# Place 1's expert read as whole fp32 values, and place 2 planned first, in a two-layer decoder trunk

## The chip, the core and the metric

The kernel runs on one core of a Trainium2 chip. A core has TensorE (PE in the rows, its weight loads PEld), VectorE (DVE), ScalarE (ACT), GpSimd (POOL) and SyncE (SP), which here issues the DMA transfers of the weights. The metric is the device time of one execution in microseconds, as a median of several runs.

## The reference: what is computed

256 tokens of width 1024 pass through two layers. Layer 0 is a recurrent mixer beside a memory attention, then a dense SwiGLU. Layer 1 is a differential attention beside a memory attention, then a mixture of experts, which is the part that the change touches:

```python
def moe_swiglu(h, w_router, w13, w2):
    logits = (xt @ w_router).astype(jnp.float32)
    top_v, top_e = lax.top_k(logits, TOP_K)          # 2 of 8 experts for each token
    gates = jax.nn.softmax(top_v, axis=-1)
    ...
    def expert_block(args):
        xb, e = args
        gu = xb @ w13[e]                              # 1024 -> 2 x 3584
        return (jax.nn.silu(gu[:, :EXPERT_DIM]) * gu[:, EXPERT_DIM:]) @ w2[e]
```

All values are fp32. An expert's w13 has 1024 x 7168 values and its w2 3584 x 1024; the eight experts together are 352 MB, and each of them is read once.

## The kernel before, in words

**Products.** TensorE takes either fp32 values or fp32r values, a shortened form of fp32. Nearly all products of weights run in fp32r: each operand is split into a high part (`hi`, ScalarE, a copy that rounds to fp32r) and a low part (`lo`, VectorE, the value minus `hi`), and the product is the sum of hi x hi, hi x lo and lo x hi. A few small products (the router, the softmax parts of layer 0 and 1, `fold`) take plain fp32 operands.

**The stream of weights (`Stream`).** Weights come in loads of 1 MB, 128 partitions x 2048 values. A load needs a raw buffer (`free`: raw0 to raw3 and, in the experts, x_hi; four `e` tiles, h3_hi and h3_lo serve once). `split` turns a load into parts and needs room for them (`room`: part0 to part4, x_lo and h1, seven places of 8 KB in a partition): one place for the high part (L124), one for the low part (L106); after the low part the raw buffer is free, and the next DMA is issued into it (L67). A place comes back when TensorE has read its piece. All this is written in program order on every engine: `split` is called whenever TensorE takes a piece, and does as many splits as there is room for at that point of the program. The first pieces of an expert's first stage are split by halves of 1024 columns (L130, L131).

**The experts.** After the router, expert 0 is place 0 (64 tokens); the other seven are ordered by their number of tokens and become places 1 to 7: place 1 has room for 128 + 8 tokens, places 2 to 4 for 128, places 5 to 7 for 64. An expert has seven blocks `j` of 512 hidden columns, each with three stages: gate `g`, up `u` (two loads each, w13) and down `w` (two loads, w2). The sequence of stages is fixed: place 0 and place 2 mixed, then place 3, then place 1 mixed with places 7, 6, 5 (about three of their stages after each of place 1's), then place 4. For places 2 to 4 the tokens are the stationary operand and the weights move, 512 columns at a time, three products (L368 to L370). For places 0, 5, 6, 7 high and low parts of 64 tokens stand side by side in one stationary operand, so two products do (L1276, L1277), and `fold` adds the halves (L1299).

**Place 1 (`run_moving`).** Here the weights are stationary and the tokens move: `xg` holds 136 high and 136 low parts side by side, so that per 128 x 128 tile of w13 one product hi x (hi, lo) of 272 columns (L1365) and one lo x hi of 136 columns (L1366) are needed. A stage has 32 such pairs, and its two loads are split as a `pair`, their pieces taken in turn. Behind them ScalarE copies one sum out of PSUM (L1370), VectorE adds the other (L1372), and SiLU (L1374) or the product with the gate (L1376) follow.

**The order at the start of the experts.** The router's transposes and products (L1005, L1008) end the attention's part; VectorE finds the top 2 (L1039 to L1068), writes the dispatch matrix of place 0 (L1086), `gather_first` collects its tokens (L1224 to L1228), and then `split` starts in earnest. The rest of the plan (`plan`: the order of the places, the dispatch matrices, the gates, the split of the tokens h3 into h3_hi and h3_lo, L1174 and L1175) is done in steps between the stages of place 0, and `gather` for place 2 follows it.

## Time and profile before

| what | value |
|---|---|
| median of 3 runs | 1576.77 us (1576.06 to 1577.21) |
| the profiled execution, its own time | 1579.21 us |
| its span | 1577.4 us |
| TensorE busy | 1533.0 us, 97% of the span |
| VectorE busy | 1239.3 us, 79% |
| ScalarE busy | 1055.8 us, 67% |
| moved by DMA | 451.60 MB, mean 286 GB/s |

TensorE's busy time counts an instruction from its start to its modelled end, and neighbours overlap; so how fast it goes is read from the distance of starts, and what it waits for from the rows that name a releaser. The experts fill the span from about 574 us to the end.

### The profile page before, as it was taken

What the parts mean: (1) busy time and instruction counts of PE and PEld (TensorE: products, weight loads), DVE (VectorE), ACT (ScalarE), POOL (GpSimd) and SP (SyncE); (2) the same over time, 40 slices, a digit from 0 to 9 for tenths busy, and PEclk for the clock granted to TensorE, in tenths of its full rate; (3) what the DMA queues carried; (4) which work ended last, traced back from release to release, by engine and by line L of the source; (5) the groups of instructions that cost most, each with busy time, mean ns of one, the idle gap of its engine ahead of it and who ended that gap; (6) DMA issues with size and microseconds to landing.
All of it is one profiled execution on the core that took longest, in us unless ns stands there. A gap on an engine that the chain in (4) does not pass through costs nothing.

```text
span 1577.4 us, 22581 instructions
## 1 busy us (share of the span) xinstructions
PE 1533.0 (97%) x8697; PEld 1300.5 (82%) x8697; DVE 1239.3 (79%) x1205; ACT 1055.8 (67%) x1142; POOL 31.9 (2%) x60
## 2 busy tenths in 40 slices
PE   8999999999999989999999999999999999999996
PEld 7988999999998857887888888887878787877774
DVE  6678654555757579888999879889899899889876
ACT  5784544444456457877887778778778787877663
POOL 0000000000000111000000000000000000000000
PEclk9999999999999999999999999999999999999998
DMA  9454655555533755999999999999999999999982
GB/s 295 161 187 161 233 183 183 183 182 197 167 128 126 265 206 194 377 377 387 395 389 352 333 324 353 356 377 377 357 339 377 371 373 353 361 371 363 333 307 98
DMA packets 218678, 451.60 MB, mean 286 GB/s; under 512 B 7241, under 2 KB 62610, under 8 KB 218562
## 3 DMA queue, kind: packets, MB, share of 16 engines
q1 hardware_dynamic: 217490, 446.76, 79.2%
q0 software_dynamic: 1072, 3.32, 0.7%
q8 instruction: 70, 1.15, 0.3%
q14 instruction: 46, 0.38, 0.1%
HBM read 449.00 MB, written 1.05 MB: 285 GB/s over the span
## 4 chain that ended last, share of the span: by engine, by line
PE 79%; DVE 10%; ACT 4%; DMA 4%; issue 2%; POOL 0%; POOLq 0%; SPq 0%; DVEq 0%; ACTq 0%
PE mm L368 11%; PE mm L370 11%; PE mm L369 11%; PE acc L369 6%; PE acc L370 6%; PE acc L368 6%; DVE part L106 5%; PE mm L1276 4%; PE mm L1277 4%; PE mm L1365 3%; DMA raw<-in_moe_w 3%; PE acc L1277 3%; PE acc L1276 3%; PE mm L1299 2%; PE mm L1255 1%
## 5 line engine op out<-in xcount | busy, mean ns | idle before, releaser
L124 ACT ACTIVATE part<-raw 128x2048 fp32r<-128x2048 f32 x188 | 359.2, 1914 | 58.9 <-DMA raw<-in_moe_w 21.6
L106 DVE TENSOR_TENSOR part<-raw,part 128x2048 fp32r<-128x2048 f32 x150 | 341.1, 2284 | 16.1 <-PE mm L370 5.5
L131 DVE TENSOR_TENSOR part<-raw,part 128x1024 fp32r<-128x1024 f32 x166 | 201.4, 1223 | 126.2 <-ACT part L130 125.6
L130 ACT ACTIVATE part<-raw 128x1024 fp32r<-128x1024 f32 x166 | 173.1, 1056 | 87.8 <-PE mm L370 47.8
L368 PE MATMUL mm<-x_hi,part 128*128 128x256 f32 x768 | 220.0, 286 | 2.1 <-ACT part L130 2.1
L370 PE MATMUL mm<-x_hi,part 128*128 128x256 f32 x768 | 218.3, 284 | 1.1 <-DVE part L131 1.1
L369 PE MATMUL mm<-x_lo,part 128*128 128x256 f32 x768 | 217.7, 283 | 0.0
L368 PEld LDWEIGHTS mm<-x_hi,part 128*128 128x128 f32 x768 | 147.9, 193 | 5.3 <-ACT part L130 2.6
L370 PEld LDWEIGHTS mm<-x_hi,part 128*128 128x128 f32 x768 | 147.8, 192 | 1.7 <-DVE part L131 1.6
L369 PEld LDWEIGHTS mm<-x_lo,part 128*128 128x128 f32 x768 | 147.8, 192 | 0.7
L1276 PE MATMUL mm<-part,xs 128*128 128x512 f32 x248 | 98.8, 398 | 0.0
L124 ACT ACTIVATE part<-x_hi 128x2048 fp32r<-128x2048 f32 x46 | 88.0, 1914 | 15.2 <-PE mm L1277 4.0
L1277 PE MATMUL mm<-part,xs 128*128 128x512 f32 x248 | 97.9, 395 | 0.0
L368 PE MATMUL mm<-part,xg 128*128 128x512 f32 x240 | 97.1, 404 | 0.0
L369 PE MATMUL mm<-part,xg 128*128 128x512 f32 x240 | 95.2, 397 | 1.8 <-DVE part L106 1.5
L370 PE MATMUL mm<-part,xg 128*128 128x512 f32 x240 | 94.7, 395 | 0.0
L106 DVE TENSOR_TENSOR part<-x_hi,part 128x2048 fp32r<-128x2048 f32 x37 | 84.5, 2285 | 7.5 <-PE mm L1365 2.5
L106 DVE TENSOR_TENSOR x_lo<-raw,h 128x2048 fp32r<-128x2048 f32 x37 | 84.6, 2285 | 5.8 <-PE mm L370 2.8
L106 DVE TENSOR_TENSOR h<-raw,part 128x2048 fp32r<-128x2048 f32 x38 | 86.8, 2284 | 1.6 <-ACT part L124 1.1
L106 DVE TENSOR_TENSOR part<-raw,x_lo 128x2048 fp32r<-128x2048 f32 x37 | 84.5, 2285 | 2.7 <-PE mm L1365 1.1
L124 ACT ACTIVATE x_lo<-raw 128x2048 fp32r<-128x2048 f32 x37 | 70.8, 1914 | 13.9 <-PE mm L1277 5.1
L1365 PE MATMUL mm<-xg,part 128*128 128x272 f32 x320 | 79.6, 335 | 0.0
(513 smaller groups left out, 3489.5 us busy)
## 6 DMA issues: line engine op xcount, KB each, us to landing
raw<-in_moe_w SPq DMA_DIRECT2D x262, 1024.0 KB, 7.3
x_hi<-in_moe_w SPq DMA_DIRECT2D x66, 1024.0 KB, 7.3
raw<-in_ffn_w SPq DMA_DIRECT2D x42, 1024.0 KB, 4.9
raw<-in_a_w_in SPq DMA_DIRECT2D x10, 1024.0 KB, 9.4
raw<-in_mem_w_kv SPq DMA_DIRECT2D x8, 1024.0 KB
raw<-in_w_kv_shared SPq DMA_DIRECT2D x8, 1024.0 KB, 6.1
raw<-in_a_w_out SPq DMA_DIRECT2D x6, 1024.0 KB, 4.8
raw<-in_b_w_q SPq DMA_DIRECT2D x6, 1024.0 KB
```

The lines of the kernel that those rows point to most:

```text
L106: nc.vector.tensor_sub(lo, src, hi.bitcast(F32))
L124: nc.scalar.activation(hi, src, AF.Copy)
L130: nc.scalar.activation(hi, src, AF.Copy)
L131: nc.vector.tensor_sub(lo, src, hi.bitcast(F32))
L368: PE.matmul(o, lhsT=l_hi, rhs=r_hi, start=start, stop=False)
L369: PE.matmul(o, lhsT=l_hi, rhs=r_lo, start=False, stop=False)
L370: PE.matmul(o, lhsT=l_lo, rhs=r_hi, start=False, stop=stop)
L1255: PE.matmul(p[:, k], lhsT=src[:, t, f], rhs=disp[:, t, g0:g0 + ng], start=t == 0, stop=t == 1)
L1276: PE.matmul(o[h], lhsT=w[:, kt], rhs=w_hi[:, i, f], start=a, stop=False)
L1277: PE.matmul(o[h], lhsT=w[:, kt], rhs=w_lo[:, i, f], start=False, stop=z)
L1299: PE.matmul(p[:, i], lhsT=src[:, i * 128:(i + 1) * 128], rhs=fold, start=True, stop=True)
L1365: PE.matmul(p[m], lhsT=w_hi[:, k, f], rhs=x_[:, kt], start=a, stop=False)
```

## The change

Four things change.

1. w13 of place 1 is not split. Its load is handed on as it is (`"raw"`), the raw buffer goes back only when the stage that reads it is over (`held`), and `xg` holds 136 fp32 values (high and low part added, ScalarE and VectorE). A pair of products becomes one fp32 product of 136 columns (L1404 after), the sums need one bank instead of two, and the copies and adds behind them go (L1370, L1372); SiLU and the product with the gate read PSUM.
2. All other loads of the experts but the first stage's are split by 2048 columns as before; the `pair` form is gone.
3. The first three pieces of place 0's first stage are split earlier, by calls written into the router's code (`upper` for the high parts between the two halves of the router's transposes, `lower` for the low parts at three points behind).
4. In `plan`, place 2's dispatch matrix, the split of h3 and place 2's gather come first; the other dispatch matrices come behind, one at a step. `hidden` has one more step between the product with the gate and the split of its result for the places of 64 tokens.

```diff
+    def upper(self):
+        src, _, whole, slot = self.piece()
+        place = self.room.popleft()
+        hi, lo = self.tiles(place, *src.shape[1:], 2)
+        self.nc.scalar.activation(hi, src, AF.Copy)
+        self.uppers.append((hi, lo, src, slot, place))
+
+    def lower(self):
+        hi, lo, src, slot, place = self.uppers.popleft()
+        self.nc.vector.tensor_sub(lo, src, hi.bitcast(F32))
...
     def split(self):
...
+            if not self.half and self.loaded[0][2] == "raw":
+                (src,), _, _, slot = self.loaded.popleft()
+                self.ready.append((src, None, (slot,)))
+                self.load()
+                continue
...
@@ stage_loads
                 else:
                     yield (rows_(moe_w13, p, k * 512, 4, j * 512 + (FFN if kind == "u" else 0), 512), 4, 512,
-                           p in moving, "pair" if p in moving else n > 0)
+                           False, "raw" if p in moving else n in big)
...
@@ the router, the top 2 and the first dispatch
             ln_tail(*ahead[1], gb, h3[:, 1])
+            st.lower()
+        else:
+            for _ in range(3):
+                st.upper()
...
     DVE.tensor_scalar(val, mb, -BIG, BIG, op0=OP.mult, op1=OP.add)
+    st.lower()
...
     dispatch((0, 0, 64), val)
+    st.lower()
...
@@ plan
+        dispatch(*PLACE[2])
+        yield
+        while st.uses(once):
+            yield
+        h3_parts.extend(hp.tile([128, 2, D], F32R, name=f"h3_{s}") for s in ("hi", "lo"))
...
+        yield from gather(4, True, blocks[2])
         for bs in PLACE.values():
             for b in bs:
-                if b[0]:
+                if b[0] not in (0, 2):
                     dispatch(b)
-            if bs[0][0] % 2:
-                yield
+                    yield
...
@@ run_moving
-        x_ = moving[0]
-        v = mw.tile([128, 4, 136], F32, name="sg")
+        x_, held = moving[0], []
+        v = s.take(2, held)
...
-            for k2 in range(2):
-                w_hi, w_lo = s.get()
-                for m in range(2):
-                    f = slice(m * 128, (m + 1) * 128)
-                    for k in range(4):
-                        a, kt = k2 == 0 and k == 0, 4 * k2 + k
-                        z = kt == KT - 1
-                        PE.matmul(p[m], lhsT=w_hi[:, k, f], rhs=x_[:, kt], start=a, stop=False)
-                        PE.matmul(p[m][:, 1], lhsT=w_lo[:, k, f], rhs=x_[:, kt, 0], start=False, stop=z)
+            for m in range(2):
+                f = slice((2 * c + m) * 128, (2 * c + m + 1) * 128)
+                for kt in range(KT):
+                    PE.matmul(p[:, m], lhsT=v[kt // 4][0][:, kt % 4, f], rhs=x_[:, kt], start=kt == 0, stop=kt == KT - 1)
...
-            for m in range(2):
-                ACT.activation(v[:, 2 * c + m], p[m][:, 1], AF.Copy)
-            for m in range(2):
-                DVE.tensor_add(v[:, 2 * c + m], v[:, 2 * c + m], p[m][:, 0])
...
+        for place in held:
+            s.back(place)
+        s.load()
```

On TensorE, at the start of place 1's first stage, the program before holds these rows (`xg` are the tokens, `part`, `h` and `x_lo` are parts of the weights; 128x272 and 128x136 are the moving columns):

```order
L1287 MATMUL mm<-ident,sg 128x128 x4
L1365 MATMUL mm<-xg,part_8206 128x272
L1366 MATMUL mm<-xg,part_8229 128x136
L1365 MATMUL mm<-xg,part_8206 128x272
L1366 MATMUL mm<-xg,part_8229 128x136
```

The changed program holds at the same place:

```order
L1329 MATMUL mm<-ident,sg 128x128 x4
L1404 MATMUL mm<-xg,raw_8082 128x136 x4
L1404 MATMUL mm<-xg,raw_8120 128x136 x4
L1404 MATMUL mm<-xg,raw_8082 128x136 x4
L1404 MATMUL mm<-xg,raw_8120 128x136 x4
L1404 MATMUL mm<-xg,raw_8082 128x136 x4
```

The products read the raw buffers themselves, one where there were two, and both loads of the stage are read from its first products to its last.

On VectorE, at the router's end, the program before holds the following rows (`val` belongs to the top 2, `disp` is place 0's dispatch matrix, `ys` its gathered tokens; L131 are the low parts of halves of a load, L106 those of whole loads):

```order
L1067 TENSOR_SCALAR val<-mb 128x16
L1068 TENSOR_TENSOR val<-val,mm 128x16
L1086 TENSOR_SCALAR disp<-slots,val 128x64 x2
L1228 TENSOR_TENSOR ys_5466<-mm,ys_5466 128x2x64 x2
L1228 TENSOR_TENSOR ys_5466<-mm,ys_5466 128x4x64
L131 TENSOR_TENSOR part_5492<-x_hi,part_5492 128x1024
L131 TENSOR_TENSOR part_5497<-x_lo,part_5497 128x1024
L131 TENSOR_TENSOR part_5500<-x_lo,part_5500 128x1024
L106 TENSOR_TENSOR h_5505<-raw_5095,part_5503 128x2048
```

And the changed program (a third L117 stands 15 rows further up, ahead of the top 2):

```order
L1100 TENSOR_SCALAR val<-mb 128x16
L117 TENSOR_TENSOR part_5369<-x_lo,part_5369 128x1024
L1102 TENSOR_TENSOR val<-val,mm 128x16
L1120 TENSOR_SCALAR disp<-slots,val 128x64 x2
L117 TENSOR_TENSOR part_5371<-x_lo,part_5371 128x1024
L1267 TENSOR_TENSOR ys_5477<-mm,ys_5477 128x2x64 x2
L1267 TENSOR_TENSOR ys_5477<-mm,ys_5477 128x4x64
L138 TENSOR_TENSOR h_5505<-raw_5095,part_5503 128x2048
```

The three low parts of half loads moved from behind the gathered tokens to three points ahead of them.

On SyncE, in the part where place 1 is mixed with the others, every DMA of the program before waits for VectorE; in the changed program two of them at each w13 stage of place 1 wait for TensorE (the DMAHW names count transfers, PE and DVE name the engine that frees the buffer):

```order
L66 DMA raw_8688<-in_moe_w 128x4x512 [waits DMAHW1_49,PE_49]
...
L66 DMA x_hi<-in_moe_w 128x4x512 [waits DMAHW2_49,PE_49]
...
L66 DMA raw_8703<-in_moe_w 128x4x512 [waits DMAHW6_49,DVE_49]
...
L66 DMA raw_8719<-in_moe_w 128x4x512 [waits DMAHW7_49,DVE_49]
...
L66 DMA raw_8740<-in_moe_w 128x2x1024 [waits DMAHW0_49,DVE_49]
```

What frees the buffers of place 1's w13 moved from VectorE's low part to the end of the stage on TensorE.

## Rows read from the trace of the kernel before

**Rows 1.** The page: the span, and the chain of work that ended last, followed back from the end, as shares of the span by engine and by line.

```profile
span 1577.4 us, 22581 instructions
...
PE 79%; DVE 10%; ACT 4%; DMA 4%; issue 2%; POOL 0%; POOLq 0%; SPq 0%; DVEq 0%; ACTq 0%
PE mm L368 11%; PE mm L370 11%; PE mm L369 11%; PE acc L369 6%; PE acc L370 6%; PE acc L368 6%; DVE part L106 5%; PE mm L1276 4%; PE mm L1277 4%; PE mm L1365 3%; DMA raw<-in_moe_w 3%; PE acc L1277 3%; PE acc L1276 3%; PE mm L1299 2%; PE mm L1255 1%
```

**Rows 2.** Busy time of each engine in four stretches (start and end in us, length, then each engine's busy time and instructions, the granted clock of TensorE, the DMA share and GB/s): the middle of the start of the experts, places 0 and 2, place 1 with 7, 6 and 5, and place 4.

```profile
592.00:616.00 24.00, 22.01 (x100) 17.51 (x100) 22.25 (x32) 16.61 (x19) 7.68 (x20) 0.86 0.26 97
626.00:813.00 187.00, 185.19 (x862) 150.35 (x861) 167.06 (x93) 149.12 (x113) 0.00 (x0) 1.00 1.03 384
937.00:1425.00 488.00, 474.16 (x2657) 398.34 (x2656) 436.40 (x342) 384.18 (x375) 2.09 (x4) 1.00 0.99 363
1425.00:1553.00 128.00, 128.00 (x554) 97.73 (x553) 110.07 (x71) 89.81 (x70) 0.00 (x0) 1.00 0.89 315
```

**Rows 3.** What TensorE waited for between 937 and 1425 us: the first and the last of the eight rows, which are fifteen waits together (us in total, times, longest).

```profile
PE acc L1277 <- DVE part L106: 4.8, 5, 1.3
...
PE acc L369 <- DVE part L106: 2.7, 4, 1.1
...
PE acc L369 <- DVE x_lo L106: 0.5, 1, 0.5
```

**Rows 4.** TensorE in order of time around one of these waits (start, duration, line; in brackets the idle time before it and what ended it).

```profile
1089.70 0.40 PE L1277 MATMUL mm<-h,xs 128*128 128x512 f32 x1
1089.93 0.40 PE L1276 MATMUL acc<-x_lo,hs 128*128 128x512 f32 x1
1091.48 0.50 PE L1277 MATMUL acc<-part,hs 128*128 128x512 f32 x1 [1.15 <-DVE part L106]
1091.82 0.40 PE L1276 MATMUL acc<-x_lo,hs 128*128 128x512 f32 x1
```

**Rows 5.** VectorE's low parts (L106) and ScalarE's high parts (L124) of whole loads between 937 and 1425 us, each as one row: busy time and number.

```profile
937.00:1425.00 488.00, 377.76 (x169) 1.00 0.99 363
...
937.00:1425.00 488.00, 319.88 (x169) 1.00 0.99 363
```

**Rows 6.** The copies and adds behind place 1's products in the same stretch (busy us, mean ns of one, idle before them).

```profile
L1372 DVE TENSOR_TENSOR sg<-sg,mm 128x136 f32<-128x136 f32 x56 | 14.6, 291 | 7.3 <-ACT sg L1370 7.2
...
L1370 ACT ACTIVATE sg<-mm 128x136 f32<-128x136 f32 x56 | 13.6, 275 | 9.2 <-PE mm L1366 9.1
```

**Rows 7.** TensorE in order of time in a stage of place 1 that waits for nothing; from the first row to the last there are eight pairs.

```profile
1084.01 0.34 PE L1365 MATMUL mm<-xg,h 128*128 128x272 f32 x1
1084.19 0.23 PE L1366 MATMUL mm<-xg,x_lo 128*128 128x136 f32 x1
...
1085.92 0.34 PE L1365 MATMUL mm<-xg,part 128*128 128x272 f32 x1
```

**Rows 8.** Products of two plain fp32 operands with a weight load each time, in order of time: the attention's weights times values, 128 moving columns, and the last expert's scatter, 512 moving columns. Each product stands as two MATMULs (x2).

```profile
511.80 0.39 PE L937 MATMUL mm<-vd,wt 128*128 128x128 f32 x2
...
513.14 0.28 PE L937 MATMUL mm<-vd,wt 128*128 128x128 f32 x1
...
1562.50 1.02 PE L1545 MATMUL mm<-us,sh 128*128 128x512 f32 x2
1563.36 1.02 PE L1545 MATMUL mm<-gs,sh 128*128 128x512 f32 x2
```

**Rows 9.** Transfers: issues between 937 and 1425 us with KB each and the median us from issue to landing; the same for the dense layer's weights over the whole span; and GB/s in 40 slices of the stretch from 590 to 616 us.

```profile
raw<-in_moe_w SPq DMA_DIRECT2D x135, 1024.0 KB, 7.2
...
raw<-in_ffn_w SPq DMA_DIRECT2D x42, 1024.0 KB, 4.9
...
GB/s 293 410 410 403 410 400 384 384 384 391 388 350 69 9 0 0 0 0 0 0 25 0 0 0 0 0 0 0 0 0 0 0 0 0 0 0 0 0 0 0
```

**Rows 10.** VectorE in order of time at the router's end (as rows 4).

```profile
564.54 0.36 DVE L1039 SCALAR_TENSOR_TENSOR lg<-mm,rstd,b_rt 128x8 f32<-128x8 f32 x2 [1.83 <-PE mm L1008]
...
569.59 0.17 DVE L1068 TENSOR_TENSOR val<-val,mm 128x16 f32<-128x16 f32 x1 [2.00 <-PE mm L1065]
...
571.68 0.29 DVE L1228 TENSOR_TENSOR ys<-mm,ys 128x128 fp32r<-128x128 f32 x1 [1.46 <-ACT ys L1227]
...
575.37 1.22 DVE L131 TENSOR_TENSOR part<-x_hi,part 128x1024 fp32r<-128x1024 f32 x1 [0.52 <-ACT part L130]
576.51 2.35 DVE L131 TENSOR_TENSOR part<-x_lo,part 128x1024 fp32r<-128x1024 f32 x2
579.07 2.29 DVE L106 TENSOR_TENSOR h<-raw,part 128x2048 fp32r<-128x2048 f32 x1 [0.20 <-ACT part L124]
```

**Rows 11.** ScalarE in order of time there.

```profile
561.90 1.09 ACT L1006 ACTIVATE vd<-mm 128x512 f32<-128x512 f32 x2 [3.30 <-PE mm L1005]
...
574.28 1.05 ACT L130 ACTIVATE part<-x_hi 128x1024 fp32r<-128x1024 f32 x1
575.23 2.00 ACT L130 ACTIVATE part<-x_lo 128x1024 fp32r<-128x1024 f32 x2
577.13 1.91 ACT L124 ACTIVATE part<-raw 128x2048 fp32r<-128x2048 f32 x1
```

**Rows 12.** What TensorE waited for between 574 and 626 us, the first and the last of seven rows.

```profile
PE mm L1277 <- DVE part L106: 3.1, 2, 2.0
...
PE mm L1276 <- ACT part L130: 0.4, 1, 0.4
```

**Rows 13.** SyncE's issues of transfers in order of time after 580 us (x4 with the time from the first to the last).

```profile
581.38 10.85 SPq L67 DMA_DIRECT2D raw<-in_moe_w  x4
615.85 0.37 SPq L67 DMA_DIRECT2D x_hi<-in_moe_w  x1
```

More of the change, by code (lines that the diff above doesn't have):

```diff
@@ L87, in uses @@
         return any(slot in slots for slot in list(self.free) + [l[3] for l in self.loaded] +
-                   ([self.half[3]] if self.half else []))
+                   ([self.half[3]] if self.half else []) + [u[3] for u in self.uppers] +
+                   [place for r in self.ready for place in r[2]])
     def tiles(self, place, n, m, parts):
@@ L95, in tiles, with piece @@
         return t.rearrange("p (s a b) -> s p a b", s=parts, a=n)
+    def piece(self):
+        todo, cols, whole, slot = self.loaded[0]
+        src = todo.pop(0)
+        if not todo:
+            self.loaded.popleft()
+        return src, cols, whole, None if todo else slot
+    def upper(self):
+        src, _, whole, slot = self.piece()
+        assert whole is False
+        place = self.room.popleft()
[5 more added lines that the diff above has]
+        self.nc.vector.tensor_sub(lo, src, hi.bitcast(F32))
+        if slot:
+            self.back(slot)
+        self.ready.append((hi, lo, (place,)))
     def split(self):
@@ L99, in split @@
         self.load()
-        while self.room and not self.hold and (self.loaded or self.half):
-            place = self.room.popleft()
+        while not self.hold and (self.loaded or self.half):
+            if not self.half and self.loaded[0][2] == "raw":
[3 more added lines that the diff above has]
+                continue
+            if not self.room:
+                break
             if self.half:
-                hi, src, cols, slot, first, whole = self.half
+                hi, src, cols, slot, first = self.half
                 self.half = None
+                place = self.room.popleft()
                 lo = self.tiles(place, *src.shape[1:], 1)[0]
@@ L108, in split @@
                 pieces = list(zip(self.halves(hi, cols), self.halves(lo, cols)))
-                pieces = [(*w, (first, place) if w is pieces[-1] else ()) for w in pieces]
-                if whole == "pair" and not self.pair:
-                    self.pair = pieces
-                else:
-                    if self.pair:
-                        pieces = [w for two in zip(self.pair, pieces) for w in two]
-                        self.pair = None
-                    self.ready += pieces
-            else:
-                todo, cols, whole, slot = self.loaded[0]
-                src = todo.pop(0)
-                if not todo:
-                    self.loaded.popleft()
+                self.ready += [(*w, (first, place) if w is pieces[-1] else ()) for w in pieces]
+            else:
+                src, cols, whole, slot = self.piece()
+                place = self.room.popleft()
                 if whole:
@@ L124, in split @@
                     nc.scalar.activation(hi, src, AF.Copy)
-                    self.half = hi, src, cols, slot, place, whole
+                    self.half = hi, src, cols, slot, place
                 else:
-                    if not todo:
-                        self.back(slot)
                     hi, lo = self.tiles(place, *src.shape[1:], 2)
@@ L139, in take @@
             for place in places:
-                self.back(place)
+                if held is None:
+                    self.back(place)
+                else:
+                    held.append(place)
         return [g[:2] for g in got]
@@ L1170, in plan @@
         yield
-        h3_parts.extend(hp.tile([128, 2, D], F32R, name=f"h3_{s}") for s in ("hi", "lo"))
-        hi, lo = h3_parts
-        for t in range(2):
-            ACT.activation(hi[:, t], h3[:, t], AF.Copy)
-            DVE.tensor_sub(lo[:, t], h3[:, t], hi[:, t].bitcast(F32))
-            yield
         for t in range(2):
```

36 lines of the change are left out of this document (25 added, 11 removed).

## The prediction, written before the changed kernel ran

> **What bounds the kernel now.** I read the chain of waits first: four fifths of it are TensorE, a tenth VectorE, and VectorE's largest part is L106, the low parts of the weights [rows 1]. The table by stretches then says where that tenth lies. Place 4 (1425 to 1553 us) has TensorE busy all the time, and nothing in the change touches it. In places 0 and 2 (626 to 813 us) TensorE is idle 187 - 185.19 = 1.8 us. In the stretch of place 1 with 7, 6 and 5 it is idle 488 - 474.16 = 13.8 us, while VectorE is busy 436.4 of 488 us, 89%, and the transfers run at 363 GB/s, under the 384 of the stretch before [rows 2]. All eight rows of TensorE's waits there name VectorE's low parts [rows 3]. So this stretch is TensorE's work, held up by VectorE now and then. The start of the experts (574 to 626 us) is the other place: TensorE waits for splits [rows 12], VectorE is busy 22.25 of 24 us in its middle, and the transfers nearly stop there, because no buffer comes free [rows 2, 13].
>
> **Place 1's products.** A pair of 272 and 136 columns takes (1085.92 - 1084.01) / 8 = 0.239 us from start to start [rows 7]. The stretch has 14 stages x 32 = 448 pairs, 107 us. Each becomes one fp32 product of 136 columns. The trace has no such shape with whole fp32 operands, but its neighbours: with 128 columns six products take 513.14 - 511.80 = 1.34 us, 0.223 us each, and with 512 columns one takes 1563.36 - 1562.50 = 0.86 us [rows 8]. In proportion to the columns 136 would be 0.228 us from the long product and 0.237 us from the short one. I take 0.237, whose shape is nearest: 448 x (0.239 - 0.237) = 0.9 us gained; the bounds are 0.9 and 5 us gained. Below nothing would need a cost that neither neighbour shows; it is a rival below.
>
> The row speaks here against the first impression, that one product for two must be a large gain: the whole product stands as two MATMULs, as the pair did, and its 512 columns take 0.86 us, nearly four times the 0.23 us of an fp32r product of 512 [rows 4]. The Trainium skill ("FP8 and Floating Point Precision", section "TensorE Precision Notes") says that true FP32 makes four passes through the array. The long product agrees (0.86 us for 4 x 512 columns), and by that rule 4 x 136 = 544 columns stand against 408 before, which speaks against the change.
>
> **What the splits cost.** 14 stages x 2 loads = 28 of the 169 loads of the stretch are no longer split. Per load VectorE spends 377.76 / 169 = 2.24 us and ScalarE 319.88 / 169 = 1.89 us [rows 5]: 62.6 and 53.0 us less. The 56 adds (14.6 us) and the 56 copies (13.6 us) go too [rows 6]; SiLU and the product with the gate stay and read PSUM. VectorE's busy time falls from 436.4 to about 359 us, 74% of the stretch, ScalarE's from 384.2 to about 318 us. More than the sum counts where it falls: before, the four parts of a place 1 stage fill four of the seven places, so that at its end only one and a half loads of the next stages stand split. After, all seven places hold the following loads, three and a half of them, and TensorE goes on while VectorE catches up.
>
> What is this worth? Only what TensorE waits: 13.8 us idle, and what each of the fifteen waits [rows 3] adds around it. In the example the starts of two products lie 1.55 us apart, where the distance before was 1089.93 - 1089.70 = 0.23 us, and the next distance is 0.34 us, 0.11 too long: 1.55 - 0.23 + 0.11 = 1.43 us lost for 1.15 us of idle time [rows 4], 0.28 us more. Fifteen times that is 4 us, together 18 us. Some waits will stay: at the rate of places 0 and 2 (1.8 us in 187) 4.7 us in 488, with their additions about 6. So I take 12 us gained in this stretch.
>
> **What it costs.** Place 1's two loads now stay in their raw buffers until the stage is over, 32 x 0.237 = 7.6 us, plus the time that TensorE takes to come to them. Only five buffers serve again and again, so three are left for transfers, and the next DMAs wait for TensorE instead of VectorE. Behind them on SyncE's queue stand the issues into buffers that VectorE frees; these free up only after the stage, since all places are full while it runs, so that the order of the queue alone delays nothing. With a transfer of 7.2 us from issue to landing when several are under way, and 4.9 us where fewer are [rows 9], and eight loads in a cycle of one place 1 stage and three others, the transfers of the next such cycle still come in time: they have about 20 us for eight loads, 8.4 MB, 411 GB/s, just above the 410 of the peaks [rows 9]; cycles with a down stage, and the gathers and scatters between, need less. So this cover is thin. The bounds of the stretch are a gain of 27 us (its 177 MB, 363 x 488, at 384 GB/s would take 461 us) and a loss of 20 us (the rival below).
>
> **The start of the experts.** The three half loads move: on ScalarE into an idle time of 3.30 us before 561.90 [rows 11], where 1.05 + 2.00 us just fit; on VectorE into gaps of 1.83, 2.00 and 1.46 us [rows 10], each longer than the 1.22 us of one. If a gap were too short, the router would be later by the rest, some tenths. The first whole split can then begin on ScalarE at 574.28 instead of 577.13, 2.85 us sooner, and VectorE, which gives the beat until 610 us, follows. Moreover, VectorE's dispatch matrices of all places but place 2, some 3 us, now stand behind ten low parts instead of between them; about 1 us of that I count, since VectorE has to do them all the same soon after. The split of h3 and place 2's gather only change their places within this part. Does the gain hold afterwards? Places 0 and 2 go at TensorE's pace with transfers at 384 GB/s, so the transfers must come sooner too: they do, since x_hi, which was issued again at 615.85 after 24 us without an issue [rows 13], is now split before the four e tiles, and the others follow the same low parts. I take 4 us, with bounds of 0 (the transfers set the pace of the next stretch) and 8 us: all TensorE's waits there, and the clock, 0.86 of full speed between 592 and 616 us, so that a part of it went at the lower of its two levels, 1.2 GHz [rows 2], after a series of waits.
>
> The additional step in `hidden` lets ScalarE do something else while VectorE finishes its product; it costs a beat of which three or more stages are left, so nothing.
>
> **The sum.** 12 + 4 + 0.9 = 17 us. The profiled execution took 1579.2 us, 2.4 us above the median of the runs; it would come to 1562 us, and the median of 1576.8 to 1560 us.
>
> **Rivals.**
> 1. The transfers set the pace of the place 1 stretch. For it speaks the DMA share of 0.99 there; against it that the stretch before moved 384 GB/s over 187 us, and the peaks 410 [rows 2, 9]. Then only the start gains: 1573 us. The Trainium skill ("DMA: Bandwidth & Descriptors", section "Where 436 GB/s comes from") puts the limit of HBM for one core at about 358 GB/s, at which this stretch would be full already; the 384 GB/s do not agree. Chance 0.14.
> 2. Slower: the held buffers starve the transfers. In the 14 stages, 14 x 7.6 = 106 us, one load at a time would be under way, 1.05 MB in 4.9 us, 214 GB/s: 22.7 MB. The other 154 MB at 384 GB/s take 402 us, so the stretch 508 instead of 488 us, and with 4 us from the start 1593 us. It decides as soon as the mean rate of the stretch falls under 363 GB/s. Against it: three buffers stay free, and a place 1 stage needs no transfer of its own while it runs. Chance 0.08.
> 3. Slower: the columns set the price. If the pair's 0.239 us were the price of 408 columns, 544 would take 0.319, and 448 x 0.08 = 36 us more; with 16 us gained elsewhere 1597 us (544 is four times 136, after the nearly four times of the long product). The 0.223 us for 4 x 128 = 512 columns speak against it: the pair is slower than its columns. The rule behind it is the Trainium skill's of four passes, named above. Chance 0.03.
> 4. More: the waits vanish altogether and the start brings its upper bound: 27 + 8 us, down to 1542 us. Chance 0.09.
>
> **How the numbers follow.** The forecast has 0.66, with its own range of 1550 to 1570. The range of 8 in 10 reaches from 1547 to 1577: it takes in rival 1 and the nearer half of rival 4, and leaves the slower ones out. A measurement of this kernel can tell 0.2% from no change, 3.2 us. Faster by more: the forecast, rival 4 and half of rival 1, 0.82; within: the other half of rival 1, 0.07; slower: rivals 2 and 3, 0.11.
>
> **What would show it.** In the profile after: L1404 with 0.23 to 0.24 us from product to product; TensorE's idle time in the stretch of place 1 at 3 to 6 us, with the low parts gone as its releaser; VectorE at about 74% there, 141 low parts; a rate above 370 GB/s; at the start, the first whole low part right behind place 0's gather, about 3 us sooner after the router than before. Wrong would be the forecast if TensorE waited for DMA in place 1's stages, or if SyncE's waits for L1404 were long and the transfers paused in them.

## The result, and the profile after

The changed kernel takes 1589.64 us (median of 4 runs, 1589.15 to 1591.57), the kernel before 1576.49 (4 runs). The ratio is 1.0081 [1.0069, 1.0093] (in brackets, here and below, the 95% interval): slower by 0.8%, where 1560 us, 1.1% faster, was predicted. The profiled executions, 1589.48 and 1579.21 us, lie 10.3 us apart, and so do their spans; the one before lies 2.7 us above its median, so the medians lie further apart, 13.2 us. One profiled execution below, that of the last run on the start, fell in a slower state (1656 us, granted clock 0.85), so its stretches are not read, and its time is the median of the other four.

Where the 10.3 us lie: place 1's first product starts at 937.3 us before and at 930.2 after, so the start of the experts gained 7.1 us. The last product of `fold`, which ends the stretch of places 1, 7, 6 and 5, starts at 1421.2 before and at 1431.5 after: the stretch grew from 483.9 to 501.3 us, by 17.4. Place 4 behind it is as long as before. The rows of these four starts, two before and two after (duration in ns, then the first and the last start in us):

```profile
L1365 PE MATMUL mm<-xg,part x320: 287/338/435, 937.3 to 1365.8; 128*128 128x272 f32 x160
L1299 PE MATMUL mm<-fold,us x208: 217/275/275, 627.1 to 1421.2; 128*128 128x64 f32 x104
```

```profile
L1404 PE MATMUL mm<-xg,raw x672: 277/279/535, 930.2 to 1377.3; 128*128 128x136 f32 x168
L1341 PE MATMUL mm<-fold,us x208: 217/275/422, 620.7 to 1431.5; 128*128 128x64 f32 x104
```

The page after: the span, the chain that ended last by engine and by line, the costliest of ScalarE's groups (busy, mean ns | idle before it and what ended most of that), place 1's products, and the transfers into the raw buffers over the whole span (number, KB, median us to landing; 7.3 us before).

```profile
span 1587.7 us, 22412 instructions
...
PE 71%; DMA 14%; DVE 7%; ACT 6%; issue 1%; POOL 0%; SPq 0%; POOLq 0%; ACTq 0%; DVEq 0%
...
L147 ACT ACTIVATE part<-raw 128x2048 fp32r<-128x2048 f32 x172 | 329.4, 1916 | 126.1 <-DMA raw<-in_moe_w 88.6
...
L1404 PE MATMUL mm<-xg,raw 128*128 128x136 f32 x672 | 85.5, 283 | 3.4 <-ACT xg L1306 3.4
...
raw<-in_moe_w SPq DMA_DIRECT2D x263, 1024.0 KB, 8.0
```

Beside [rows 1], the transfers' share of the chain went from 4% to 14% and TensorE's from 79% to 71%. The engine that stands idle for transfers is not TensorE but ScalarE, whose high part is the first step of a split (L147 after, L124 before).

The stretches after, with the columns of [rows 2]: places 0 and 2, place 1 with 7, 6 and 5, place 4.

```profile
619.00:806.00 187.00, 185.42 (x867) 151.11 (x867) 169.67 (x100) 150.58 (x115) 6.50 (x20) 1.00 1.03 387
...
930.00:1435.00 505.00, 477.87 (x2655) 402.53 (x2654) 363.51 (x258) 325.65 (x291) 2.09 (x4) 0.98 0.96 351
1435.00:1563.00 128.00, 128.00 (x554) 97.73 (x553) 110.10 (x72) 89.37 (x71) 0.00 (x0) 1.00 0.89 315
```

VectorE fell from 436.4 us (89% of the stretch) to 363.5 (72%), as the change meant it to, and TensorE is idle for 27.1 us instead of 13.8. The DMA share fell from 0.99 to 0.96 together with the rate, from 363 to 351 GB/s: the DMA engines were not slower, they had less to do. The exact stretch moved 351 x 501.3 = 176 MB; at the 387 GB/s of places 0 and 2 these would take 455 us.

What the engines waited for between 930 and 1435 us: ScalarE and VectorE first, then SyncE's queue, then TensorE (us, times, longest).

```profile
ACT part L147 <- DMA raw<-in_moe_w: 69.5, 50, 5.9
DVE part L138 <- ACT part L147: 45.3, 24, 5.5
ACT part L147 <- DMA x_hi<-in_moe_w: 21.4, 13, 5.9
ACT x_lo L147 <- DMA raw<-in_moe_w: 18.2, 11, 5.6
ACT h L147 <- DMA raw<-in_moe_w: 17.9, 10, 6.4
...
SPq L66 <- DVE part L138: 218.9, 83, 4.9
SPq L66 <- PE mm L1404: 7.7, 9, 2.7
...
PE mm L1341 <- ACT us L1475: 5.7, 3, 4.2
PE acc L1319 <- DVE part L138: 5.5, 2, 2.9
PE mm L1385 <- ACT y_hi L1378: 4.9, 2, 4.0
```

The first row's counterpart before, between 937 and 1425 us:

```profile
ACT part L124 <- DMA raw<-in_moe_w: 3.3, 8, 0.8
```

From 3.3 to 69.5 us, and VectorE waits behind ScalarE for another 45.3. TensorE names small works of ScalarE and, as in [rows 3], VectorE's low parts, but no transfer; so the rows nearest to the loss do not name its cause, and it has to be followed back two steps. The chain does that. After, in order of time (start, us, what):

```profile
1044.67 7.73 DMA raw<-in_moe_w
1052.48 1.92 ACT part L147
1054.42 2.30 DVE part L138
1056.74 4.89 DMA raw<-in_moe_w
1061.71 1.92 ACT part L147
1063.66 2.30 DVE part L138
1065.98 10.91 DMA raw<-in_moe_w
1076.97 1.92 ACT x_lo L147
```

This is a closed loop: transfer, high part, low part, buffer free, next transfer into it. It turns only as fast as there are buffers to turn it. In this part of it stands a stage of place 1:

```profile
1052.70 7.57 PE L1404 MATMUL mm<-xg,raw 128*128 128x136 f32 x64
```

The same time as stretches (columns of [rows 2]): before this stage, its two halves, and two rows behind it.

```profile
1047.50:1052.50 5.00, 5.00 (x26) 4.13 (x26) 1.88 (x2) 0.02 (x1) 0.00 (x0) 1.00 1.05 386
1052.50:1056.50 4.00, 4.00 (x35) 3.96 (x34) 2.08 (x1) 3.21 (x2) 0.00 (x0) 1.00 0.83 324
1056.50:1060.30 3.80, 3.80 (x34) 3.80 (x33) 3.09 (x4) 3.29 (x4) 0.00 (x0) 1.00 0.67 209
1060.30:1064.30 4.00, 4.00 (x18) 3.19 (x18) 2.59 (x2) 2.48 (x3) 0.00 (x0) 1.00 0.92 317
1064.30:1070.00 5.70, 5.12 (x31) 4.17 (x30) 3.87 (x2) 3.25 (x3) 0.00 (x0) 1.00 1.05 390
```

The rate falls from 386 to 209 GB/s while the stage holds its two buffers, and is back 4 us after its end. Against 386 the three middle rows lack 62 x 4.0 + 177 x 3.8 + 69 x 4.0 = 1197 GB/s x us, 1.2 MB, or 3.1 us of transfer.

Over the 14 stages of place 1 together, each from its first product to its last, the transfers moved 277 GB/s (33.5 MB in 121 us), between 217 and 375 in a single one; before, over the same stages, 374. In 7 of the 14 the transfers into the two buffers given back are issued only 2.1 to 4.9 us after the stage's end, behind an issue that waits for VectorE.

How the missing transfers reach TensorE, the chain shows ahead of the longest wait for `y_hi` (4.0 us), the high part of a finished place's result:

```profile
1280.24 12.16 DMA raw<-in_moe_w
1292.48 1.91 ACT part L147
...
1297.70 1.91 ACT part L147
1299.61 0.53 ACT y_hi L1378
```

ScalarE waits for a load and splits it and two more, and the small work for which TensorE waits stands behind these splits.

### The profile page after: what moved, and what is told of

It is laid out like the page before. It is cut to its first block, busy times and chain, and to the rows that moved or that the text cites. A ratio compares the mean times of both kernels' runs of the same rounds, so it can differ in the third digit from the quotient of the medians.

```text
span 1587.7 us, 22412 instructions
## 1 busy us (share of the span) xinstructions
PE 1532.3 (97%) x8697; PEld 1303.4 (82%) x8697; DVE 1166.5 (73%) x1129; ACT 993.6 (63%) x1050; POOL 30.8 (2%) x60
## 3 DMA queue, kind: packets, MB, share of 16 engines
HBM read 449.00 MB, written 1.05 MB: 283 GB/s over the span
## 4 chain that ended last, share of the span: by engine, by line
PE 71%; DMA 14%; DVE 7%; ACT 6%; issue 1%; POOL 0%; SPq 0%; POOLq 0%; ACTq 0%; DVEq 0%
PE mm L396 10%; PE mm L398 10%; PE mm L397 10%; DMA raw<-in_moe_w 10%; PE acc L396 6%; PE acc L397 6%; PE acc L398 6%; DVE part L138 4%; PE mm L1318 4%; PE mm L1319 4%; ACT part L147 3%; PE mm L1404 2%; DMA x_hi<-in_moe_w 2%; PE acc L1319 2%; PE acc L1318 2%; DMA raw<-in_a_w_in 2%
## 5 line engine op out<-in xcount | busy, mean ns | idle before, releaser
L147 ACT ACTIVATE part<-raw 128x2048 fp32r<-128x2048 f32 x172 | 329.4, 1916 | 126.1 <-DMA raw<-in_moe_w 88.6
L138 DVE TENSOR_TENSOR part<-raw,part 128x2048 fp32r<-128x2048 f32 x139 | 316.6, 2287 | 56.2 <-ACT part L147 40.3
L147 ACT ACTIVATE part<-x_hi 128x2048 fp32r<-128x2048 f32 x42 | 80.4, 1915 | 33.7 <-DMA x_hi<-in_moe_w 23.2
L138 DVE TENSOR_TENSOR x_lo<-raw,h 128x2048 fp32r<-128x2048 f32 x34 | 77.7, 2286 | 19.0 <-ACT h L147 9.5
L1404 PE MATMUL mm<-xg,raw 128*128 128x136 f32 x672 | 85.5, 283 | 3.4 <-ACT xg L1306 3.4
L1404 PEld LDWEIGHTS mm<-xg,raw 128*128 128x128 f32 x672 | 83.2, 193 | 4.9 <-ACT xg L1306 3.8
L147 ACT ACTIVATE x_lo<-raw 128x2048 fp32r<-128x2048 f32 x36 | 69.0, 1916 | 28.9 <-DMA raw<-in_moe_w 20.8
L138 DVE TENSOR_TENSOR part<-x_hi,part 128x2048 fp32r<-128x2048 f32 x32 | 73.2, 2287 | 13.7 <-ACT part L147 10.6
```

What stands on the lines that cost most here:

```text
L138: nc.vector.tensor_sub(lo, src, hi.bitcast(F32))
L147: nc.scalar.activation(hi, src, AF.Copy)
L1404: PE.matmul(p[:, m], lhsT=v[kt // 4][0][:, kt % 4, f], rhs=x_[:, kt], start=kt == 0, stop=kt == KT - 1)
```

## The experiments

**Theory A:** the held buffers. A w13 stage of place 1 keeps two of the five recurring raw buffers from the landing to its last product, and the transfers starve. **Theory B:** the order of the work. Since w13 of place 1 takes no places, all seven fill with splits of loads that lie further ahead (a longer lookahead), and the small works of the stages stand behind these splits on ScalarE and VectorE. **Theory C:** the whole fp32 products, and their reads of the raw buffers, slow the transfers themselves. The rows above show that A and B can act together; how much each is worth, the runs must say. Other questions were what the start gained by, and whether the relief of VectorE is worth what was predicted. "Stretch" below is place 1's first product to the last of `fold`: 483.9 us before, 501.3 after.

**Each half of the change alone.** First everything but the whole fp32 loads (place 1 split as a pair, as before):

```diff
-                           False, "raw" if p in moving else n in big)
+                           p in moving, "pair" if p in moving else n in big)
```

> The change without its first part: place 1's w13 is split in pairs as before; the early half loads, the order of the plan and the step in hidden are kept. The stretch is counted from place 1's first product to the last fold (484 us before, 501 us after). Theory A (the held raw buffers starve the transfers) and B (the splits stand further ahead in the engines' order and block them) and C (whole fp32 products and their reads slow the transfers) all expect the start to keep its 7 us and the stretch to return to 482 to 486 us: 1568 to 1571 us. Rival D: the stretch is bound by transfers anyway and gives the start's gain back: 1575 to 1577 us.

1564.29 us, ratio 0.9917 [0.99, 0.9933]. Place 1 starts at 930.0 us and its stretch takes 476.6, 7.3 less than before and less than the 482 to 486 that A, B and C expected; the step in `hidden`, below, accounts for 5.1 us of that. The rival D, which had the transfers give the start's gain back, is out.

Then the whole fp32 loads alone, in the kernel before:

```diff
-                           p in moving, "pair" if p in moving else n > 0)
+                           False, "raw" if p in moving else n > 0)
```

> The kernel before with nothing but place 1's whole fp32 w13 and tokens. A, B and C: place 1 starts at 937 us as before and the stretch is about 501 us, so 1591 to 1595 us. If the loss came from the new order of the plan or the step in hidden, the stretch would be at or under 484 us and the time 1570 to 1577 us.

1600.92 us, 1.015 [1.0124, 1.0176]; place 1 starts at 937.3 as before, and the stretch takes 507.3 us, more than the 501 expected: 6.0 us above the changed kernel's, about what the step in `hidden` is worth. So the two halves have opposite signs, and the whole loss is the fp32 loads': 507.3 - 483.9 = 23.4 us in the kernel before, 501.3 - 476.6 = 24.7 us in the changed one.

**The buffers given back at once.** In the changed kernel a whole load is copied, as fp32, into one of the seven places, and its raw buffer is free again; the products read the place.

```diff
             if not self.half and self.loaded[0][2] == "raw":
                 (src,), _, _, slot = self.loaded.popleft()
-                self.ready.append((src, None, (slot,)))
+                place = self.room.popleft()
...
+                self.nc.scalar.activation(t, src, AF.Copy)
+                self.back(slot)
+                self.ready.append((t, None, (place,)))
```

> The changed kernel, but each whole fp32 load of place 1 is copied by ScalarE into one of the seven places, and its raw buffer goes back after the copy instead of after the stage; the products are the same, ScalarE has 53 us more, VectorE nothing. A: the transfers keep their five buffers, and the waits for low parts stay away: stretch 468 to 478 us, 1555 to 1565 us. B (the splits still stand far ahead, one place per load instead of two) and C (same products): stretch 495 us and more, 1583 us and more.

1556.38 us, 0.9871 [0.9854, 0.9887]. The stretch takes 465.4 us, 35.9 less than with held buffers, although each of the 28 loads has a copy more. The profiled execution, 1553.52 us, is the fastest of the four; by the medians the two kernels lie 33.3 us apart. Its row over the exact stretch (columns of [rows 2]):

```profile
929.80:1395.20 465.40, 459.80 (x2637) 390.66 (x2636) 359.47 (x256) 370.04 (x316) 1.61 (x3) 1.00 1.01 376
```

The DMA share is 1.01 again, the rate 376 GB/s, and TensorE is idle for 5.6 us. Over the 14 stages of place 1 the transfers move 397 GB/s, where the held buffers left 277. The parked loads take places, though, so this run shortens the lookahead too; alone it does not part A from B.

**One buffer held.** The first load of each stage is copied into a place, the second stays in its raw buffer.

```diff
+            raw = not self.half and self.loaded[0][2] == "raw"
+            if raw and self.raws % 2:
+                (src,), _, _, slot = self.loaded.popleft()
+                self.ready.append((src, None, (slot,)))
```

> The changed kernel with the first load of each place 1 stage copied to a place by ScalarE, and the second held in its raw buffer to the stage's end. With both held the stretch was 501 us, with both copied 465 us. A (the loss grows with the buffers held): one held buffer lies between, 474 to 490 us, 1563 to 1579 us. If the loss came from the products reading the raw buffers or from SyncE's queue waiting for TensorE as such, half of the reads and waits stay and the stretch is 490 us or more: 1579 us or more.

1568.13 us, 0.9942 [0.9925, 0.9959]; the stretch takes 478.6 us. None, one and two held buffers give 465.4, 478.6 and 501.3 us: 13.2 us for the first, 22.7 for the second. That is A's band; the reads from raw buffers or SyncE's waits for TensorE as such would have left 490 us or more. Over the 14 stages the rates are 397, 377 and 277 GB/s.

```profile
931.60:1410.20 478.60, 467.67 (x2637) 397.84 (x2636) 361.75 (x255) 345.73 (x304) 1.60 (x3) 0.98 1.00 366
```

**Six raw buffers, two of them held.** In the changed kernel the place x_lo serves as a sixth recurring raw buffer, so that six places are left.

```diff
-    st.free += [(xr, "x_hi", True), (xr, "x_lo", st.room)]
+    st.free += [(xr, "x_hi", True), (xr, "x_lo", True)]
```

> The changed kernel with x_lo as a sixth raw buffer instead of a seventh place; the held loads stay held. A: four buffers instead of three are left to the transfers while place 1's stage runs, so half of the loss of 17 us or more returns: stretch 484 to 493 us, 1572 to 1582 us. C: no difference, 1588 to 1592 us. B: one place less is also half a load less of lookahead, a gain of a quarter at most: 1585 us or more.

1573.71 us, 0.9974 [0.9961, 0.9986]. The missing place costs the earlier places: place 1 starts at 943.4 us, 13.2 later than after. But its stretch takes 473.8 us, 27.5 less, with both loads held as in the changed kernel:

```profile
943.40:1417.20 473.80, 463.75 (x2638) 391.25 (x2636) 362.75 (x255) 322.45 (x290) 1.61 (x3) 1.00 1.01 372
```

Four buffers are free during a stage here, as in the run before, and the two stretches lie 4.8 us apart; over the 14 stages the transfers move 354 GB/s. Theory C is out: the products and their reads are those of the changed kernel. The rest speaks for A, but the gain is larger than A expected (484 to 493 us). A place fewer is also a shorter lookahead, so B is not out by this run alone, and no run shows what a sixth buffer brings without held loads.

**A shorter lookahead, two buffers held.** While whole loads wait or are read, four places stay out of use, as the four parts of a stage took them before.

```diff
-            if not self.room:
+            if len(self.room) <= 4 * bool(self.raws):
                 break
```

> The changed kernel, but while whole loads of place 1 wait or are read, four of the seven places are kept out of use, so that the splits stand no further ahead in the order of ScalarE and VectorE than in the kernel before. B (the splits far ahead block ScalarE): the stretch returns to 490 us or less, 1578 us or less. A (the held buffers): nothing is gained, and as the loads behind must wait longer in their raw buffers, the stretch is 501 us or more, 1589 to 1610 us.

1583.69 us, 1.0036 [1.0022, 1.0049]; the stretch takes 494.9 us, which neither theory expected (490 or less, 501 or more). B gets 6.4 of the 35.9 us (by the medians 6.0 us of the kernel's time), and the DMA share stays at 0.96:

```profile
928.40:1423.30 494.90, 468.09 (x2637) 389.64 (x2636) 364.41 (x256) 327.50 (x291) 1.59 (x3) 1.00 0.96 355
```

Over the 14 stages of place 1 the transfers move 249 GB/s, even less than the 277 after, so the gain lies between the stages. And it is a net figure: the shorter lookahead also brings TensorE's waits for low parts back. The largest (the view runs from 930 to 1419 us):

```profile
PE mm L1320 <- DVE part L139: 14.3, 10, 2.6
```

So the order alone may be worth more than 6.4 us. But a run with one place fewer and a sixth buffer got back 27.5, one with four places fewer 6.4: the number of free buffers carries most of the loss, the order a smaller part whose exact share stays open.

**One buffer fewer, nothing else.** In the kernel before, x_hi serves once only, so four recurring buffers are left.

```diff
-    st.free += [(xr, "x_hi", True), (xr, "x_lo", st.room)]
+    st.free += [(xr, "x_hi", False), (xr, "x_lo", st.room)]
```

> The kernel before with x_hi as a buffer that serves once, so that four raw buffers serve again and again instead of five; nothing is held. A: a load keeps its buffer 4.9 to 7.2 us for the transfer and 4.2 us for the two splits, with four buffers 2.3 to 2.9 us a load against 484 / 169 = 2.86 us now; so the buffers become the bound: the transfers' rate in the stretch falls under 355 GB/s and the time is 1590 to 1620 us. If the number of buffers is not what the transfers live on: 1574 to 1580 us.

1631.61 us, 1.0327 [1.0293, 1.036]: 54 us more, beyond the 1590 to 1620 expected. In the profiled execution, 1642.58 us and so 11 above the median, place 1 starts 18.5 us later (955.8), and its stretch takes 528.9 us, 45.0 more:

```profile
955.80:1484.70 528.90, 488.00 (x2639) 405.48 (x2637) 436.04 (x338) 385.25 (x372) 1.60 (x3) 0.97 0.94 332
```

So four buffers are too few for the kernel before, without any fp32 load.

**What the start gained by.** The extra step in `hidden` alone, in the kernel before:

```diff
                     DVE.tensor_mul(h, h, p)
                 yield
+            yield
             hd = b.room([128, 4, 128], F32R, "hs")
```

> The kernel before with only the additional step in hidden. The run without the first part of the change had a stretch of 477 us against 484; if the step makes that, ScalarE's wait for the product with the gate (26 us in the stretch before) goes and the stretch is 476 to 479 us: 1569 to 1572 us. If it does nothing (what the prediction said), 1575 to 1578 us, and the 7 us came from the plan's order or the early halves.

1570.33 us, 0.9948 [0.9929, 0.9966]. Place 1 starts at 933.6 us, 3.7 sooner, and the stretch takes 478.8 us, 5.1 less. What it takes away is a wait of ScalarE for VectorE's product between 574 and 1421 us, 25.2 us in the kernel before, and 0.3 us with the step:

```profile
ACT hs L1307 <- DVE sh L1303: 25.2, 19, 2.8
ACT part L124 <- DMA raw<-in_moe_w: 21.6, 36, 1.6
```

```profile
ACT part L124 <- DMA raw<-in_moe_w: 35.4, 50, 2.8
...
ACT hs L1308 <- DVE sh L1303: 0.3, 1, 0.3
```

Most of the 25 us turn into ScalarE's waits for transfers: all its rows that name a load come to 56.3 us with the step, to 34.5 before (the largest of each is shown). 7.0 us of the kernel's time are the gain.

Then the change without the fp32 loads, and with the plan's old order (the edit against the run without the fp32 loads):

```diff
-        dispatch(*PLACE[2])
...
-        yield from gather(4, True, blocks[2])
         for bs in PLACE.values():
             for b in bs:
-                if b[0] not in (0, 2):
+                if b[0]:
                     dispatch(b)
```

> The run without the first part of the change, with the plan in its old order as well; the early half loads and the step in hidden stay. If the start's 7 us come from the early halves, place 1 starts at 930 to 931 us and the time is 1564 to 1566 us; if half of it comes from the plan's order (dispatch matrices behind the low parts), at 933 to 934 us, 1567 to 1569 us.

1570.49 us, 0.9945 [0.9924, 0.9966], against 1564.29 with the new order. Place 1 starts at 934.3 us against 930.0, so the order is worth about 4 us of start. The ratios' intervals overlap, but the starts agree: the six profiles with the new order and seven places begin place 1 at 928.4 to 931.7 us, those with the old order at 937.3, or at 933.6 and 934.3 with the step. Between 574 and 626 us (columns of [rows 2]) before, after, and with the old order:

```profile
574.00:626.00 52.00, 43.60 (x198) 33.16 (x198) 47.39 (x59) 43.95 (x45) 10.78 (x25) 0.93 0.53 187
```

```profile
574.00:626.00 52.00, 46.28 (x235) 36.92 (x235) 47.07 (x54) 44.79 (x45) 7.72 (x9) 1.00 0.61 221
```

```profile
574.00:626.00 52.00, 45.89 (x213) 36.99 (x213) 45.74 (x57) 43.47 (x43) 10.58 (x25) 0.90 0.57 198
```

Here the granted clock is 1.00 with place 2's gather ahead, and with the old order a part of the 52 us goes at 1.2 GHz. But other runs with the new order show 0.93 to 0.97 in the same 52 us, the one with the copy on VectorE (below) for example:

```profile
574.00:626.00 52.00, 46.28 (x219) 36.92 (x218) 45.17 (x52) 42.29 (x42) 5.99 (x9) 0.93 0.59 203
```

It begins place 1 at 931.7 us all the same. So a part of the clock in the gain is not shown.

Last, the change without the fp32 loads and without the early half loads:

```diff
             ln_tail(*ahead[1], gb, h3[:, 1])
-            st.lower()
-        else:
-            for _ in range(3):
-                st.upper()
```

> The run without the first part of the change, and without the early half loads: new order of the plan and step in hidden only. The run with the old plan and early halves began place 1 at 934.3 us, the run with the step in hidden alone at 933.6 us, the one with all three at 930.0 us. If the early halves bring nothing once the step is there, this one begins at 929 to 931 us and takes 1563 to 1566 us; if they bring the 2.85 us of the prediction, it begins at 932.5 to 934 us and takes 1566 to 1569 us.

1566.45 us, 0.9937 [0.9921, 0.9954], 2.2 us above the 1564.29 with them; place 1's start, by which the expectation decides, can't be read. The intervals of the two ratios overlap, and at the old order the early halves show nothing (1570.49 with them, 1570.33 without, both with the extra step). What they are worth, 0 to 2 us, stays open.

**The version that beats both.** As with the buffers given back at once, but VectorE, which has the time now, makes the copy (the edit against that run):

```diff
-                self.nc.scalar.activation(t, src, AF.Copy)
+                self.nc.vector.tensor_copy(t, src)
```

> The run that copies whole loads into places, with the copy on VectorE instead of ScalarE: ScalarE 53 us less in the stretch, VectorE more by 28 copies. If neither engine bounds the stretch any more (both under 80% busy there), nothing changes: 1553 to 1559 us. If VectorE's queue is still what the low parts come late from, its 28 copies bring waits back: 1560 us or more.

1554.48 us, 0.9853 [0.9836, 0.9869], 23 us under the kernel before; its stretch takes 464.8 us. That it is better than the copy on ScalarE is not shown, since the intervals overlap. The expectation's condition, both engines under 80% busy, is not met: VectorE is at 84%, and its copies cost nothing that shows.

```profile
931.70:1396.50 464.80, 459.49 (x2637) 390.54 (x2636) 388.46 (x281) 322.39 (x290) 1.58 (x3) 1.00 1.02 376
```

## Why the prediction was wrong, step by step

**The step that failed** is "What it costs". It gave the held buffers no price in the forecast: "the transfers of the next such cycle still come in time", about 20 us for eight loads at 411 GB/s, "just above the 410 of the peaks". A cover that needs the peak rate for its whole length is none. The step took the loads of a cycle as something to be caught up between two stages, but there is little rate to catch up with: the stretch before place 1 shows 384 GB/s, behind a stage the rate is 390, and the kernel with parked loads needs 376 in the mean. The step also had "the order of the queue alone delays nothing", "since all places are full while it runs"; but the stage at 1052.70 us had a split's low part in it (1054.42), and buffers given back lay idle up to 4.9 us, behind another issue. In place of nothing the runs show 35.9 us (501.3 against 465.4 with the buffers given back; 33.3 by the medians), of which the shorter lookahead alone got back 6.4. An estimate from the rows comes near this: at 387 GB/s instead of 277 over the 121 us of the 14 stages, 13.3 MB more would have come, 34 us of transfer.

**Rival 2 is what happened**, with a chance of 0.08. Its mechanism was right, its size partly by luck. It had one load at a time under way in a stage, 214 GB/s for 7.6 us, 1.3 MB short; the stage above shows 209 GB/s in its second half and 1.2 MB short around it, but over the 14 stages the rate was 277, and outside them about 375 instead of its 384. It gave a stretch of 508 us and 1593 us in all; 501.3 (507.3 without the rest of the change) and 1589.6 were measured. Its point of decision, a mean rate under 363 GB/s, was passed with 351. "Three buffers stay free, and a place 1 stage needs no transfer of its own" was no argument against it: the stages behind do need them, and four buffers are too few already, as the run with four shows.

**The relief of the splits** was there. With the buffers given back the stretch falls from 476.6 to 465.4 us, 11.2 (7.9 by the medians), where 12 + 0.9 were predicted, and VectorE's busy time came out at 359.5 us against 359. But the sum hides a shift: 3.6 of the 11.2 are the products (next), and TensorE's idle time falls only from 11.1 to 5.6 us, since the step in `hidden` and the rest of the change had taken some of the 13.8 before. The held buffers took the gain three times over: -11.2 + 35.9 = 24.7 us.

**Place 1's products** cost less than the 0.237 us taken. The 64 MATMULs of a stage, two to a product, take 7.57 us with the last one's 0.28: (7.57 - 0.28) / 31.5 = 0.231 us a product, so 448 x (0.239 - 0.231) = 3.6 us are gained instead of 0.9, within the bounds. Rival 3 falls with it: it had 0.319 us. Its four times 136 columns in 0.231 us are 2.35 columns a nanosecond at a granted clock of 2.4 GHz, close to one a cycle. The four passes of the Trainium skill ("FP8 and Floating Point Precision", section "TensorE Precision Notes") agree with this row. The mistake of the rival was to price the columns by the pair, whose 408 in 0.239 us are only 1.71 a nanosecond.

**The start** gained 7.1 us, within the bounds of 0 to 8 but above the 4 taken, and for other reasons than those named. The extra step in `hidden`, costed at nothing, gives 3.7 us at place 1's start; the plan's order some 4 us, where "about 1 us" was counted; the half loads, the main reason given, 0 to 2 us, although they did what was said of them: the first whole low part starts at 576.78 us instead of 579.07 [rows 10]. That the gain stayed within the bounds is thus luck in part. The parts do not add up exactly, since each fills gaps that another leaves.

**`hidden`'s step** was the second mis-sized term: "so nothing" is 7.0 us of the kernel's time. ScalarE was busy only 79% of the stretch [rows 2], yet taking 25 us of its waits away shortened the kernel. The likely path is that the high part of a split stands behind the waiting instruction, and by it the next transfer is late; ScalarE's waits for transfers, which rise in their place, fit this, but no run shows it by itself.

**Rival 1**, the transfers as the pace with only the start gained, falls in its strict form: the kernel with parked loads moved 376 GB/s over the same stretch. The limit of about 358 GB/s that the Trainium skill names ("DMA: Bandwidth & Descriptors", section "Where 436 GB/s comes from") does not agree with the 387 GB/s of places 0 and 2 either. What set the pace of the changed kernel was the supply of buffers, not the rate of the memory.

**Of the marks to look for**, the two that were to show the forecast wrong did not: TensorE's waits name no transfer, and SyncE's wait for L1404 stayed short, 7.7 us in all, although the held buffers are the cause. Issues stand in program order, and the queue books its time on whichever buffer it waits for next, mostly VectorE's. Behind the stage that ends at 1060.27 us:

```profile
1060.17 0.37 SPq L66 DMA_DIRECT2D x_hi<-in_moe_w  x1
1062.28 4.08 SPq L66 DMA_DIRECT2D raw<-in_moe_w  x4
```

The issues into the two buffers that the stage gave back are the second and third of the four (1062.90 and 1063.51 us); when their turn comes, the buffers have long been free. The 141 low parts and the 0.23 us of a product came as forecast. What showed the failure were TensorE's idle time (27.1 us where 3 to 6 were expected), the rate (351 GB/s where over 370 was), and ScalarE's wait for DMA.

## What to carry to other kernels

Before a load is kept in its landing buffer for longer, multiply: the buffers that are left over the time of one turn (landing, split, release) must still give the rate that the stretch needs, and not only its peak; if they do not, a copy into a second place can be cheaper (here 28 copies against 35.9 us). Here three buffers of 1.05 MB over the 9.1 to 11.4 us of landing and two splits give 276 to 346 GB/s, under the 363 of the stretch. The sum of the pieces is still too kind: with four buffers it gives 368 to 461 GB/s, and 332 were measured, 12.6 us a turn, so the turn is better measured as a whole. An engine at 89% and a stream of transfers at 0.99 may be two limits one behind the other: relieving the first at the expense of the second loses. And an engine that is not full still delays what is queued behind its waiting instruction, so a wait is costed by who stands behind it.

## What the runs showed of the hardware

- The time of a transfer from issue to landing depends on what else is under way: almost alone in a stage of place 1 a load of 1 MB took 4.89 us, 214 GB/s; behind the stage, when several buffers come free at once, 10.91. The median in the stretch went from 7.2 us [rows 9] to 8.2 while the mean rate fell, so a longer landing time was no sign of a faster stream.
- A product of whole fp32 values with 136 moving columns takes 0.231 us, less than in proportion to the 0.223 us of 128 columns (0.237), and near that of the 512 columns (0.228).
- The granted clock of a short stretch was no sign of the program's order: between 574 and 626 us it was 0.90 to 0.97 in the five profiles with the old order of the plan, and 0.93 to 1.00 in the seven with the new one.
- What keeps buffers slowed the transfers: over the 14 stages of place 1 they moved 397 GB/s with no buffer held, 377 with one of five held, 277 with two of five, and 354 with two of six.
